# A trunk of two layers on eight cores: instructions listed a second time by due dates, squares summed on VectorE, pooling by running sums, conditioning rows ahead of x

## The chip, the cores and the metric

The kernel runs on the 8 cores of one Trainium2 chip. Each core takes one of the 8 sequences; the cores don't talk to each other. The time is the device time in microseconds (us) of the slowest core. Most executions agree within 0.3%. In some, pairs of cores, or all cores of a die, have stretches in which TensorE's granted clock is lowered, and the run is longer: 2094.3 us against 2070 for the kernel before. Below, a run is called undisturbed if no core had such a stretch; only such runs, or undisturbed cores of a run, are compared, unless the text says otherwise.

## The reference, cut to what matters

```python
for l in range(DEPTH):                                  # 2 layers; x is (8, 2048, 1024) float32
    mod = c_act @ w_mod[l] + b_mod[l]                   # shift, scale, gate for three sub-layers
    h, gate = modulate(x, norm_g[l, 0], mod_f1)         # rmsnorm(x) * g * (1 + scale) + shift
    x = x + 0.5 * gate * swiglu(h, w_ffn_in[l, 0], w_ffn_out[l, 0])    # 1024 -> 2 x 2816 -> 1024
    h, gate = modulate(x, norm_g[l, 1], mod_mx)
    y = mixer_ab(h, ...) if l % 2 == 0 else mixer_pool(h, pool_w_grp[j], pool_scale[j])
    x = x + gate * y
    h, gate = modulate(x, norm_g[l, 2], mod_f2)
    x = x + 0.5 * gate * swiglu(h, w_ffn_in[l, 1], w_ffn_out[l, 1])
return rmsnorm(x, final_g)

# mixer_pool, per channel group i with window w = 2, 4, 8, 16 (256 channels each):
p = ((cum - shifted(cum, w)) / min(t + 1, w)) - h       # trailing mean minus the token itself
outs.append(p @ w_grp[i])
```

## The kernel before

x lies transposed in SBUF (channels on partitions) as four tiles of 512 tokens. The sub-layers work on two tiles at a time, `p` = 0 and 1 in turn. The gate and up projections of the SwiGLU run as a Strassen-like scheme of 7 products, which needs sums of blocks of h ("h sums") and of the weights ("weight sums"); VectorE makes both. While one pair of tiles is in the last down projection, the next pair's h is built.

A small scheduler in the kernel decides the order. Every instruction is added with an estimated cost; on TensorE it goes behind the last one, on the other engines into the first gap that fits. Each engine is then given its instructions in the order of their planned starts, with semaphores between engines. In the traces of before, the records of VectorE (2575, accumulator reads left out) and of ScalarE (1494) stand in the order of the program on all eight cores, but for 5 memsets on VectorE whose records begin up to 0.07 us behind those of the next instruction.

```python
class Sched:
    def add(self, eng, fn, reads=(), writes=(), cost=0.1, dma=None, nbytes=0, after=0.0):
        ...                                   # dependencies from the keys read and written
        t = self.tl[e].find(ready, c)         # append for "pe", first gap for the others
        ...
    def emit(self, nc, block):
        order = sorted(ops, key=lambda o: (o.start, o.idx))
```

The norm needs the sum of squares over channels: ScalarE squares, GpSimd adds two squared channel blocks, TensorE sums over partitions with a matrix of ones. In the last down projection this follows each finished pair of channel blocks.

```python
def square_pair(c, t):
    qs = [sq_rot.next(), sq_rot.next()]
    for i, q in enumerate(qs):
        act(SQ[:, q, :], Xv(c + i, t), AF.Square, ...)
    z = sp_rot.next()
    op = add("pool", I("tensor_tensor", out=SP[:, z, :], in0=SQ[:, qs[0], :], in1=SQ[:, qs[1], :], op=ALU.add), ...)
    return z, op.end + 0.3
```

The norm factor, `rstd`, is ScalarE's Ln and Exp, just before h is built:

```python
elif nxt is not None:
    rstd(other, after=Sd.tl["pe"].tail())
    run_down(dn, rest, build_h(nxt))          # h: X * RS on VectorE, scale and shift on ScalarE, then h sums
    carry.append(lambda dn=dn: bg_add(dn.rest_ones()))
```

At the start, x comes first, then 16 rows of the first sub-layer's conditioning weights, each 128 x 1024 float32. Each is worked off on TensorE by 8 matmuls with one column (16 records in the profile):

```python
for kc in range(NC):
    op = add("pe", I("matmul", PS[b][:, i:i + 1], ap[:, kc * 128:(kc + 1) * 128], CT[:, kc:kc + 1], ...), ...)
```

The pooling multiplies h by the group's weights and then by band matrices of 128 x 128:

```python
mm(PS[bk][:, n * 128:(n + 1) * 128], GTv[:, m, dd * 128:(dd + 1) * 128], BAND0v[i] if first else BANDv[i], ...)
if not first:
    mm(PS[bk][:, n * 128:(n + 1) * 128], prev, BPREVv[i], False, True, ...)
```

In the profiles every line of the program is that of one helper (L323 before, L432 after, with other numbers in two experiments), so groups are told apart by tile names: H is h, SLOTS the weights, ACTB the hidden activations, X the residual, TP scratch, SQ and SP squares and their sums, WMOD rows of conditioning weights, RS the norm factor, ps PSUM.

## Time and profile before

| | before |
|---|---|
| time, median of the fast runs | 2070 us |
| span of the slowest core | 2066.1 us |
| TensorE busy | 1999.7 us, 97% |
| VectorE busy | 1470.1 us, 71% |
| GpSimd busy | 329.1 us, 16% |
| first feed-forward matmul, median of the cores | 81.6 us |
| from there to the start of the last projection matmul | 1962.1 us |
| from there to the end | 20.2 us |

The last three rows are read from the records of the eight cores. They cut the span into a start, a middle and an end. In the middle a second number is useful. A 512-column matmul that streams without a gap starts 0.216 us after the one before it, one of 256 columns 0.109, one of 128 columns 0.056. What the start-to-start times hold beyond that is called lost below: 43 us in the middle of the kernel before (median of the cores), 39 of them later than 12 us after the first feed-forward matmul. The first 12 us are left out because TensorE is at half clock there at first: on all eight cores of before the first matmuls start 0.43 us apart, and where the records have the stretch, a granted clock of 0.50 lasts until 84.6 to 91.1 us. Where TensorE falls back to half clock after a wait, the slower matmuls count as lost too: on core 1 of before, behind waits of 3.0, 3.3 and 4.4 us, the granted clock is 0.50 for 3.4, 3.4 and 6.8 us, and matmuls start 0.43 us apart. And where a core's record lacks matmuls (20 to 36 of them, on two cores of most profiles), each gap counts 0.216 us too much, so the ranges below leave such cores out.

### The profile page before, as it was taken

Reading aid. Unit: us, or ns where it says so; the run is one execution under the profiler, and the core shown is the slowest. Engines: PE = TensorE matmul, PEld = TensorE weight load, DVE = VectorE, ACT = ScalarE, POOL = GpSimd, SP = SyncE. Lnnn points to the kernel's source line nnn. Section 1 sums busy time; section 2 is a strip of 40 time slices with the busy share of each in tenths; the row PEclk is TensorE's granted clock in tenths of the full one; section 3 lists DMA queues with packets and bytes.
Section 4 is the critical chain, followed back from the end, with each engine's and each line's share of the span. In section 5 each row is a group of like instructions: output and inputs, shape, how many; then the busy total and the mean of one; then the engine's idle time right before and its main releaser. Section 6 shows DMA issues by size and latency. Waiting matters only on the chain.

```text
span 2066.1 us, 26542 instructions; the slowest of 8 cores (2061.0 to 2066.1 us)
## 1 busy us (share of the span) xinstructions
PE 1999.7 (97%) x9586; PEld 954.3 (46%) x9586; DVE 1470.1 (71%) x2831; ACT 922.6 (45%) x1522; POOL 329.1 (16%) x431
## 2 busy tenths in 40 slices
PE   6999999999999989999999999999999999999996
PEld 5744444444545434444444444444454445444442
DVE  2584888677888885769677976696687766685654
ACT  3351555236353453255314641464376545564242
POOL 2101221002213120012001200120012101220001
PEclk9999999999999999999999999999999999999998
DMA  8597666866575746554767485636344453436552
GB/s 256 108 226 162 136 130 145 171 134 138 131 144 124 150 80 121 141 99 87 154 136 144 102 181 140 108 62 105 59 72 81 73 98 55 84 63 111 139 86 82
DMA packets 71391, 248.78 MB, mean 120 GB/s; under 512 B 7136, under 2 KB 7264, under 8 KB 70752
## 3 DMA queue, kind: packets, MB, share of 16 engines
q0 software_dynamic: 46928, 153.63, 45.3%
q1 hardware_dynamic: 24336, 93.45, 13.5%
q8 instruction: 80, 1.31, 0.3%
q14 instruction: 47, 0.39, 0.1%
HBM read 392.29 MB, written 8.39 MB: 194 GB/s over the span
## 4 chain that ended last, share of the span: by engine, by line
PE 83%; DVE 13%; DMA 2%; POOL 1%; ACT 1%; issue 0%; SPq 0%; DVEq 0%; POOLq 0%
PE ps L323 83%; DVE X L323 4%; DVE TP L323 3%; DVE H L323 2%; DVE SLOTS L323 2%; DMA WMOD<-wmod 1%; POOL SP L323 1%; DVE WMOD L323 1%; DMA X<-xT 1%; ACT H L323 0%; ACT SQ L323 0%; DVE ps L323 0%; DVE ACTB L323 0%; ACT L323 0%; DVE MODT L323 0%
## 5 line engine op out<-in xcount | busy, mean ns | idle before, releaser
L323 PE MATMUL ps<-H,SLOTS 128*128 128x512 f16 x5440 | 1207.0, 380 | 17.5 <-DVE X L323 12.7
L323 PEld LDWEIGHTS ps<-H,SLOTS 128*128 128x128 f16 x5440 | 530.8, 98 | 653.0 <-issue 34.8
L323 PE MATMUL ps<-ACTB,SLOTS 128*128 128x512 f16 x3072 | 687.0, 380 | 3.2 <-DVE X L323 2.1
L323 ACT ACTIVATE ps<-ps 128x512 f32<-128x512 f32 x528 | 307.0, 583 | 666.2 <-PE ps L323 665.8
L323 PEld LDWEIGHTS ps<-ACTB,SLOTS 128*128 128x128 f16 x3072 | 300.8, 98 | 363.7 <-issue 9.4
L323 DVE TENSOR_TENSOR ACTB<-TP,ps 128x512 f16<-128x512 f32 x368 | 251.9, 687 | 105.4 <-PE ps L323 74.0
L323 DVE SCALAR_TENSOR_TENSOR X<-ps,GH,X 128x512 f32<-128x512 f32 x320 | 232.0, 746 | 132.4 <-PE ps L323 131.6
L323 DVE TENSOR_TENSOR SLOTS<-SLOTS 128x512 f16<-128x512 f16 x704 | 310.1, 459 | 10.8 <-DMA SLOTS<-win 0.9
L323 ACT ACTIVATE TP<-ps 128x512 f32<-128x512 f32 x400 | 238.8, 597 | 172.3 <-PE ps L323 171.9
L323 DVE TENSOR_TENSOR TP<-ps,TP 128x512 f32<-128x512 f32 x176 | 121.6, 691 | 205.9 <-ACT ps L323 205.6
L323 POOL DMA_DIRECT2D SLOTS<-win x176 | 95.3, 541 | 978.7 <-PE ps L323 923.8
L323 POOL TENSOR_TENSOR SP<-SQ 128x512 bf16<-128x512 f32 x112 | 153.3, 1373 | 252.3 <-ACT SQ L323 236.3
L323 ACT ACTIVATE SQ<-X 128x512 f32<-128x512 f32 x224 | 133.6, 622 | 118.0 <-DVE X L323 104.3
L323 DVE SCALAR_TENSOR_TENSOR WMOD<-WMOD,CB 128x512 f32<-128x512 f32 x256 | 177.6, 723 | 2.6 <-DMA WMOD<-wmod 2.5
L323 ACT ACTIVATE H<-TP,MODT,AS 128x512 f16<-128x512 f32 x160 | 122.1, 804 | 102.0 <-DVE TP L323 66.1
L323 DVE TENSOR_TENSOR ps<-ps,TP 128x512 f32<-128x512 f32 x176 | 122.9, 699 | 32.7 <-PE ps L323 32.4
L323 DVE TENSOR_TENSOR TP<-X,RS 128x512 f32<-128x512 f32 x192 | 135.9, 743 | 5.5 <-ACT H L323 4.2
L323 POOL DMA_DIRECT2D SLOTS<-wout x64 | 45.5, 710 | 334.6 <-PE ps L323 334.6
L323 PE MATMUL ps<-SP,ONES 128*128 128x512 bf16 x122 | 48.6, 417 | 29.6 <-POOL SP L323 27.1
L323 DVE TENSOR_TENSOR H<-H 128x1024 f16<-128x1024 f16 (+1 forms) x72 | 56.7, 807 | 1.6 <-ACT H L323 0.6
L323 PEld LDWEIGHTS ps<-SP,ONES 128*128 128x128 bf16 x122 | 12.5, 103 | 57.9 <-issue 49.7
L323 ACT ACT_TABLE_LOAD x28 | 35.9, 1283 | 1.5 <-PEq L329 1.1
(72 smaller groups left out, 534.2 us busy)
## 6 DMA issues: line engine op xcount, KB each, us to landing
SLOTS<-win POOLq DMA_DIRECT2D x176, 512.0 KB, 5.5
WMOD<-wmod SPq DMA_DIRECT2D x134, 512.0 KB, 5.8
SLOTS<-wout POOLq DMA_DIRECT2D x32, 768.0 KB, 7.2
SLOTS<-wout POOLq DMA_DIRECT2D x32, 640.0 KB, 6.9
SLOTS<-wab POOLq DMA_DIRECT2D x28, 512.0 KB, 7.1
X<-xT SPq DMA_DIRECT2D x4, 2048.0 KB, 16.1
outT<-X SPq DMA_DIRECT2D x16, 512.0 KB, 4.4
ACTB<-wmod SPq DMA_DIRECT2D x10, 512.0 KB, 19.1
```

Source lines behind the costliest of these rows:

```text
L323: return lambda E: getattr(E, name)(*a, **k)
```

## The change

Its intent is to start the feed-forward work earlier, to take the norm's work out of the crowded ends of the sub-layers, to have less to do on TensorE in the pooling, and to order VectorE's and ScalarE's instructions by how urgently TensorE needs them. The diff, cut to its core:

```diff
+    def relist(self, free=("dve", "act")):
+        ...
+            due.append(o.start + (0.0 if o.eng == "pe" else 8.0))
+        for o in reversed(ops):               # a due date is the earliest of the users', less cost and latency
+            ...
+        # second listing: DVE and ACT take the ready instruction with the earliest due date;
+        # PE, GpSimd and SP keep their order
     ...
-        op = add("pool", I("tensor_tensor", out=SP[:, z, :], in0=SQ[:, qs[0], :], in1=SQ[:, qs[1], :], op=ALU.add), ...)
+    def squares(c, t, n):                     # SQ is bf16 now, n squares, n/2 sums in one instruction
+        ...
+        op = tt_(SQ[:, q:q + h, :], SQ[:, q:q + h, :], SQ[:, q + h:q + n, :], ALU.add, ...)
     ...
-        for c0 in (0, 2):                     # build_h
-            for c in (c0, c0 + 4, c0 + 1, c0 + 5):
-                for tt in range(2):
+        for tt in range(2):
+            for n, c in enumerate((0, 4, 1, 5, 2, 6, 3, 7)):
     ...
-                    rstd(other, after=Sd.tl["pe"].tail())
-                    run_down(dn, rest, build_h(nxt))
-                    carry.append(lambda dn=dn: bg_add(dn.rest_ones()))
+                    run_down(dn, rest, side)  # side = build_h(nxt), begun with the end of the gate stage
+                    carry.append(lambda p=p: bg_add(stats_gen([2 * p, 2 * p + 1])))
     ...                                       # rstd: half a sub-layer earlier where possible
+    on_pe = (0, 2, 4, 6, 8, 10, 12, 14, 15)   # the other 7 rows: one scalar_tensor_tensor of 1024 columns on DVE
+    early = 6                                 # six rows are sent ahead of x
     ...
-    for s, k in zip(range(NSLOT), (0, 2, 4, 5, 6, 7)):
+    for s, k in zip(range(NSLOT), (3, 5, 6, 7, 7, 7)):    # first weight pieces
     ...                                       # pooling
-    mm(... GTv[:, m, ...], BAND0v[i] if first else BANDv[i], ...); mm(... prev, BPREVv[i], ...)
+    add("dve", I("tensor_tensor_scan", sv, PMH[:, c, cols], PMH[:, c, 16 - w + tt * TT:16 - w + (tt + 1) * TT],
+                 init, ALU.add, ALU.subtract), ...)
+    op = stt(out, PMH[:, c, cols], -float(w), sv, ALU.mult, ALU.add, ...)
+    mm(PS[bk][:], PMW[...], PMD[:, kc, tt * TT:(tt + 1) * TT], ...)      # 512 columns
```

Also, the value projection of the spatial mixer uses 512 columns in place of 256, and background work is started only while VectorE's planned backlog is under 2 us.

## The prediction

> **What bounds the kernel now.** I read the page's busy shares, then the table of stretches (5 us at the start, 50 us over the whole span), then the timeline of both ends, then the groups of instructions.
>
> ```profile
> span 2066.1 us, 26542 instructions; the slowest of 8 cores (2061.0 to 2066.1 us)
> PE 1999.7 (97%) x9586; PEld 954.3 (46%) x9586; DVE 1470.1 (71%) x2831; ACT 922.6 (45%) x1522; POOL 329.1 (16%) x431
> ```
>
> TensorE is busy 97%, so at first sight only 66 us can be won. The stretches say more (core 1; the number in brackets behind PE counts matmuls):
>
> ```profile
> 150.00:200.00 50.00, 48.64 (x226) 21.84 (x224) 25.49 (x51) 4.11 (x7) 3.38 (x6) 1.00 0.87 191
> 200.00:250.00 50.00, 46.66 (x207) 20.11 (x205) 36.32 (x71) 28.34 (x51) 14.25 (x15) 0.97 0.52 107
> 300.00:350.00 50.00, 47.05 (x210) 20.79 (x209) 45.37 (x94) 26.75 (x45) 8.65 (x10) 0.97 0.58 127
> 700.00:750.00 50.00, 42.31 (x180) 17.65 (x178) 46.34 (x74) 30.90 (x50) 15.22 (x13) 0.93 0.46 84
> 1000.00:1050.00 50.00, 50.00 (x234) 22.66 (x232) 31.74 (x67) 11.16 (x19) 4.26 (x7) 1.00 0.76 161
> 1150.00:1200.00 50.00, 46.92 (x217) 20.66 (x215) 46.86 (x91) 28.26 (x48) 11.17 (x12) 1.00 0.57 127
> ```
>
> An undisturbed stretch starts 233 to 234 matmuls in 50 us, 0.215 us each: TensorE streams without a gap. What other stretches lack is lost time. At the ends of sub-layers VectorE is busy 45 to 47 of 50 us and TensorE waits for it. The deficits (7, 26, 23, 53 and 16 above, and 4 to 12 in each of some five other stretches) come to about 175 matmuls, 38 us; with 3 us in the mixer, where widths mix, 41 us. The 53 are the boundary behind the spatial mixer.
>
> The start and the end, from the timeline:
>
> ```profile
> 12.74 2.19 ACT L323 ACTIVATE SQ<-X 128x512 f32<-128x512 f32 x4 [9.74 <-DMA X<-xT]
> 26.21 3.41 PE L323 MATMUL ps<-CT,WMOD 128*128 128x1 f32 x16
> 77.27 3.55 PE L323 MATMUL ps<-CT,WMOD 128*128 128x1 f32 x16
> 81.55 1.91 PE L323 MATMUL ps<-H,SLOTS 128*128 128x512 f16 x4
> 85.08 45.28 PE L323 MATMUL ps<-H,SLOTS 128*128 128x512 f16 x197 [1.63 <-DVE SLOTS L323]
> ...
> 2048.06 1.26 POOL L323 TENSOR_TENSOR SP<-SQ 128x512 bf16<-128x512 f32 x1 [3.27 <-ACT SQ L323]
> 2050.68 10.69 DVE L323 SCALAR_TENSOR_TENSOR X<-X,SM,RS 128x512 f32<-128x512 f32 x16 [3.36 <-ACT RS L323]
> 2052.16 9.62 SPq L323 DMA_DIRECT2D outT<-X  x8
> ```
>
> The first feed-forward matmul starts at 81.6 us. Before it TensorE is "busy" from 26 to 81 with one-column fp32 products, 16 rows of the conditioning weights at 3.4 us a row: the largest reserve, invisible in the busy share. At the end 16 final scalings run one behind another.
>
> ```profile
> 10.00:15.00 5.00, 0.00 (x0) 0.00 (x0) 0.00 (x0) 2.19 (x4) 1.03 (x1) 1.00 1.02 328
> 25.00:30.00 5.00, 4.37 (x21) 4.18 (x20) 0.65 (x3) 3.05 (x5) 1.87 (x5) 1.00 1.02 348
> 55.00:60.00 5.00, 5.00 (x26) 5.00 (x25) 1.22 (x4) 0.46 (x1) 0.00 (x0) 1.00 0.05 19
> ```
>
> The DMA engines are full until 30 us and nearly idle at 55 us: the rows wait for TensorE, not the reverse.
>
> [...] the matmuls from 81.6 us are 0.43 us apart, and core 4's granted clock is 0.50 up to 90 us. The new kernel pays this too. [...] the product of two SBUF operands below averages 743 ns, the one with a PSUM operand 691.
>
> ```profile
> L323 DVE TENSOR_TENSOR TP<-X,RS 128x512 f32<-128x512 f32 x192 | 135.9, 743 | 5.5 <-ACT H L323 4.2
> L323 POOL TENSOR_TENSOR SP<-SQ 128x512 bf16<-128x512 f32 x112 | 153.3, 1373 | 252.3 <-ACT SQ L323 236.3
> L323 DVE TENSOR_TENSOR H<-H 128x1024 f16<-128x1024 f16 x56 | 50.1, 914 | 0.7
> L323 PE MATMUL ps<-WMOD 128*128 128x256 f16 x128 | 19.2, 273 | 0.0
> L323 PE MATMUL ps<-PMC,WMOD 128*128 128x128 f16 x240 | 19.1, 219 | 0.0
> ```
>
> **The change, part by part.**
>
> *Start (rows ahead of x, 7 of 16 rows on VectorE).* TensorE's rows fall to 9 x 3.4 = 31 us, half of them while x is still arriving. The bound becomes the DMA: 16 rows of 0.52 MB, x tiles of 2 x 2.1 MB and 0.6 MB of small inputs are 13.2 MB, at the 328 GB/s of the first stretches 40 us, plus 4 us for start and landing. Two or three weight pieces, released by earlier rows, come between: each reads 1.05 MB, 3.2 us, so 6 to 9 us if all stand ahead of the last row. I take half, 4 us: last row at 48. Then its own product, 3.4 us, and scale, h and h-sum, some 3 us: first matmul near 54 in place of 81.6. Gain 27.5 us (22 to 33).
>
> *Pooling by running sums.* Started without gaps, a 512-column matmul takes 0.216 us, 256 columns 0.109, 128 columns 0.056 (start-to-start times in the trace). Removed: 128 x 0.109 + 248 x 0.056 = 27.8 us of TensorE. Added: 64 x 0.216 = 13.8. Gain 14.0 us, straight on TensorE's stream. The value projection at 512 instead of 256 columns is worth 0.2.
>
> VectorE pays: [...] 24 subtractions at 0.75, 8 at 0.43: 51 us, in two sub-layer halves.
>
> *Squares on VectorE.* GpSimd's 112 additions of 1.37 us go. VectorE gets 48 additions of 1024 columns at 0.81 to 0.91 us, about 41 us, and 8 short ones. With 7 rows at 1.35 us, less dropped constants (10) and less contention (20, guessed from 743 against 691), VectorE has about 1470 + 51 + 41 + 3 + 10 - 30 = 1545 us, 77% of the new span. It fits on average.
>
> *Background statistics, early norm, listing by due dates.* These aim at the 41 us of boundary losses. Squares and their sums leave the crowded down projection; the norm factor is computed half a sub-layer earlier; h is built tile by tile beginning some 8 us earlier; conditioning rows no longer stand in front of urgent evictions. Left over, by judgement: first sub-layer 12.4 to 4 us, feed-forward into mixer 2.8 to 2, behind the mixer 11.7 to 4 (some 34 us of VectorE work against 27.6 us of output projection, so it cannot vanish), five later boundaries 14.3 to 6. Together 41 to 16, gain 25.
>
> *End.* Listing by due date pulls the first tile's factor and its 8 scalings (8 x 0.67 = 5.3 us) before the last projection; VectorE's addition (0.43) replaces GpSimd's 1.26. About 5.5 us.
>
> Sum: 2066.1 - 27.5 - 14.2 - 25 - 5.5 = 1993.9 us of span. Times lie 3.6 us above the span (2069.66 against 2066.1): 1997 us.
>
> **Rivals.**
>
> *VectorE becomes the bound in the pooling stages.* From the down projection at 1448 to the end of the gate stage at 1565 it is busy some 77 of 117 us. 25 us of scans and subtractions and 3 of squares, with the stretch 7 us shorter, make 105 of 110. If background work is not done by then it is drained in a lump before the boundary, up to 8 us in each of two stages: about 2012.
>
> *The start's gain is given back.* Six weight pieces lay ready at 81 us before; now hardly two. From 54 to 170 us the DMA must bring weights, gate rows and the late x; it has room, but tightly. A starved first sub-layer would return 8 to 12 us: about 2008.
>
> *The list is wrong on the chip.* It reckons 0.62 us where the trace has 0.69 to 0.75. Engines run strictly in list order, so a wrong order makes new waits. Losses would stay near 40: about 2022. Against it: the old list used the same costs and lost little in steady stretches.
>
> **Range and chances.** The start may miss by 6 us, the losses by -10 to +25: 1980 to 2022 holds it 8 times in 10. 2% faster is 2028, beyond all three rivals alone; two together would reach it. Faster 0.91, same 0.08, slower 0.01.
>
> **What would show it.** Right: first feed-forward matmul at 50 to 60 us with a full DMA until then; no 128-column matmuls; stretches over 230 matmuls at the late boundaries; VectorE near 77%; fewer than 16 scalings after the last matmul. Wrong: a start later than 65 us, TensorE waiting on weight DMAs between 60 and 170 us, VectorE at 95% and over 5 us lost near either pooling stage, or as many missing matmuls at the boundaries as before.

## The result, and the profile after

| | before | after | difference |
|---|---|---|---|
| time, median | 2070.09 us | 1984.93 us | -85 us |
| start: first feed-forward matmul | 81.6 | 59.0 | -22.6 |
| middle | 1962.1 | 1910.1 | -52.0 |
| end | 20.2 | 13.2 | -7.0 |
| lost in the middle, without its first 12 us | 39.1 | 3.2 | -35.9 |

The ratio is 0.9591, with a 95% interval of 0.9572 to 0.961. Ratios here are the mean time of one kernel's fast runs over that of the other's of the same rounds, so they are not quite the ratio of the medians. The lower four rows are medians of the eight cores of the two profiled runs. Start, middle and end sum to 81.6 us and not to 85: the slowest core gains 1.6 us more than the median one, and the time lay 3.6 us above the slowest span before and 1.6 after. The middle's 52 us are these 36 us, 2 us of the first 12, and 14 us of matmuls that no longer exist.

The page of the kernel after, its span and busy shares:

```profile
span 1982.8 us, 25298 instructions; the slowest of 8 cores (1981.7 to 1982.8 us)
PE 1947.8 (98%) x9042; PEld 896.8 (45%) x9042; DVE 1462.9 (74%) x2930; ACT 909.6 (46%) x1503; POOL 171.0 (9%) x306
```

VectorE's busy time has fallen a little, although it took on scans, subtractions, squares' sums and rows. That is the first thing to explain. The table of stretches after, in the columns of the prediction's table (stretch, its length, then busy us and number of instructions of TensorE's matmuls, its weight loads, VectorE, ScalarE and GpSimd, then granted clock, share of the DMA engines, GB/s). The second line holds the boundary behind the spatial mixer, where 53 matmuls were missing, and the third a pooling stage:

```profile
650.00:700.00 50.00, 49.44 (x230) 22.25 (x229) 48.11 (x96) 31.79 (x51) 4.24 (x8) 1.00 0.66 127
700.00:750.00 50.00, 49.19 (x229) 22.12 (x227) 42.92 (x108) 24.12 (x41) 4.80 (x8) 1.00 0.91 192
1650.00:1700.00 50.00, 50.00 (x233) 22.64 (x232) 49.02 (x90) 29.16 (x49) 4.09 (x7) 1.00 0.39 67
```

Of the other stretches from 100 to 1950 us, one in the spatial mixer (550 to 600) has 230 matmuls; the rest have 232 or more, up to 257 where narrow ones are among them. VectorE may be busy 49 of 50 us without TensorE losing a single matmul: what counts is what stands first in its queue.

Both ends of the timeline after (core 2):

```profile
52.02 3.55 PE L432 MATMUL ps<-CT,WMOD 128*128 128x1 f32 x16
57.61 0.21 DVE L432 SCALAR_TENSOR_TENSOR AS<-ps,SB,SM 128x1 f32<-128x1 f32 x1
58.77 16.44 PE L432 MATMUL ps<-H,SLOTS 128*128 128x512 f16 x64
...
1972.39 0.38 PE L432 MATMUL ps<-SQ,ONES 128*128 128x512 bf16 x1 [1.84 <-DVE SQ L432]
1974.19 5.39 DVE L432 SCALAR_TENSOR_TENSOR X<-X,SM,RS 128x512 f32<-128x512 f32 x8 [1.94 <-ACT RS L432]
```

The last row's product ends at 55.6 us, but VectorE turns it into the scale only at 57.6, because other instructions stand before it in its list (it is busy 5.00 of 5 us from 55 to 60). At the end 8 scalings are left in place of 16.

The groups of instructions after, to be held against those of before (count, then busy time and mean ns of one):

```profile
L432 DVE TENSOR_TENSOR SLOTS<-SLOTS 128x512 f16<-128x512 f16 x704 | 281.2, 418 | 9.6 <-DMA SLOTS<-win 3.2
L432 DVE TENSOR_TENSOR TP<-X,RS 128x512 f32<-128x512 f32 x192 | 125.4, 682 | 14.5 <-ACT RS L432 11.8 <-ACT H L432 2.4
L432 DVE TENSOR_TENSOR H<-H 128x1024 f16<-128x1024 f16 x56 | 37.2, 681 | 0.1
L432 DVE TENSOR_TENSOR SQ<-SQ 128x1024 bf16<-128x1024 bf16 x48 | 33.0, 687 | 10.9 <-ACT SQ L432 10.7
L432 DVE TENSOR_TENSOR_SCAN WMOD<-PMH,SLAST 128x512 f32<-128x512 f16 x18 | 23.0, 1277 | 0.0
```

The same weight sums took 459 ns on average before, the same product of x and norm factor 743, the same h sum 914. Nothing in these instructions changed, only what ran beside them. The line of the weight sums before, and a place in the timeline that shows how a mean of 459 comes about:

```profile
L323 DVE TENSOR_TENSOR SLOTS<-SLOTS 128x512 f16<-128x512 f16 x704 | 310.1, 459 | 10.8 <-DMA SLOTS<-win 0.9
...
708.21 0.75 DVE L323 SCALAR_TENSOR_TENSOR X<-ps,GH,X 128x512 f32<-128x512 f32 x1
708.69 1.27 POOL L323 TENSOR_TENSOR SP<-SQ 128x512 bf16<-128x512 f32 x1 [4.15 <-ACT SQ L323]
708.87 1.37 DVE L323 TENSOR_TENSOR SLOTS<-SLOTS 128x512 f16<-128x512 f16 x1
```

The weight sum starts while GpSimd is adding, and lasts 1.37 us in place of 0.42. I went through all records of core 1. Of the 704 weight sums, 51 overlap an addition on GpSimd and take 0.95 us on average, at most 2.36; the other 653 take 0.420. The h sums of 1024 columns take 1.22 against 0.685, the products of x and factor 1.02 against 0.68, the row products 1.52 against 0.68. All of these have two operands in SBUF. Instructions with one operand in PSUM weren't held up: 0.685 overlapping against 0.687 free, and 0.743 against 0.746. Summed over the four groups, (0.53 x 51) + (0.54 x 24) + (0.33 x 34) + (0.83 x 12) = 61 us of VectorE's time before. These additions stood in the last down projection, where h is built.

These 61 us aren't the whole answer. All durations on VectorE's list of core 1, added up, rose from 1592 to 1618 us: some 99 us of new work against 63 us won in the four groups and 10 us of dropped work. The busy time counts overlapping records once, and 33 us more of them overlap now.

### The profile page after: what moved, and what is told of

Read it like the earlier page. It is cut to its first block, busy times and chain, and to the rows that moved or that the text cites. A ratio compares the mean times of both kernels' runs of the same rounds, so it can differ in the third digit from the quotient of the medians.

```text
span 1982.8 us, 25298 instructions; the slowest of 8 cores (1981.7 to 1982.8 us)
## 1 busy us (share of the span) xinstructions
PE 1947.8 (98%) x9042; PEld 896.8 (45%) x9042; DVE 1462.9 (74%) x2930; ACT 909.6 (46%) x1503; POOL 171.0 (9%) x306
## 4 chain that ended last, share of the span: by engine, by line
PE 94%; DMA 2%; DVE 2%; SPq 1%; ACT 0%; issue 0%; DVEq 0%; POOLq 0%
PE ps L432 94%; DMA ACTB<-wmod 1%; SPq L432 1%; DVE TP L432 1%; DMA WMOD<-wmod 1%; DMA SLOTS<-win 1%; DVE WMOD L432 0%; DVE ACTB L432 0%; DVE X L432 0%; DVE SLOTS L432 0%; ACT ps L432 0%; ACT H L432 0%; ACT PMH L432 0%; DVE H L432 0%; ACT RS L432 0%
## 5 line engine op out<-in xcount | busy, mean ns | idle before, releaser
L432 PE MATMUL ps<-ACTB,SLOTS 128*128 128x512 f16 x3072 | 676.2, 379 | 1.0 <-DVE ACTB L432 1.0
L432 DVE TENSOR_TENSOR SLOTS<-SLOTS 128x512 f16<-128x512 f16 x704 | 281.2, 418 | 9.6 <-DMA SLOTS<-win 3.2
L432 ACT ACTIVATE SQ<-X 128x512 bf16<-128x512 f32 x224 | 133.3, 623 | 199.0 <-DVE X L432 117.6
L432 DVE SCALAR_TENSOR_TENSOR WMOD<-WMOD,CB 128x512 f32<-128x512 f32 (+1 forms) x258 | 173.6, 690 | 7.0 <-DMA WMOD<-wmod 7.0
L432 DVE TENSOR_TENSOR TP<-X,RS 128x512 f32<-128x512 f32 x192 | 125.4, 682 | 14.5 <-ACT RS L432 11.8
L432 PE MATMUL ps<-SQ,ONES 128*128 128x512 bf16 x130 | 43.4, 422 | 14.1 <-ACT SQ L432 5.8
L432 DVE TENSOR_TENSOR SQ<-SQ 128x1024 bf16<-128x1024 bf16 (+1 forms) x56 | 36.3, 649 | 13.7 <-ACT SQ L432 13.5
L432 ACT ACTIVATE PMH<-TP,MODT,AS 128x512 f16<-128x512 f32 x32 | 25.5, 809 | 40.5 <-DVE TP L432 40.3
L432 DVE TENSOR_TENSOR H<-H 128x1024 f16<-128x1024 f16 (+1 forms) x72 | 43.4, 623 | 0.2
```

The lines of the kernel that those rows point to most:

```text
L432: return lambda E: getattr(E, name)(*a, **k)
```

## The experiments

Theory V: the boundary losses went because VectorE got its time back: GpSimd's additions no longer hold it up, and the squares left the crowded stage. Theory L: they went because of the order by due dates. The start and the pooling are tested by themselves. Where a run gave "lost", it is the middle without its first 12 us, on undisturbed cores. All runs gave correct results. The first seven kernels and a repetition ran on a chip where pairs of cores often had a stretch of lowered clock, so their ratios have wide intervals and I quote undisturbed executions; there the kernel before gave 2068.9 to 2070.1 us.

**Without the second listing.** One line is taken out of the changed kernel.

```diff
-    Sd.relist()
```

> The changed kernel without the second listing: every engine keeps the order of the first listing. Theory L (the due-date order is what removed the boundary losses of about 38 us): most of them come back, and the early last scalings go too; 2010 to 2025 us. Theory V (VectorE has room now, because GpSimd's additions no longer hold it up and the squares left the down projection): the first order does nearly as well; under 1993 us, with under 8 us lost between the first feed-forward matmul and the last projection.

Measured: 2003.7 to 2005.4 us, 20 us more than the change; ratio 0.9657 (0.954 to 0.9774). Lost 16.7 us, and the end is 20.9 us long, with 16 scalings in one piece again. Neither theory's number holds. The listing is worth some 13.5 us in the middle and 7.7 at the end, on top of everything else. But without it, 22 of the 36 us in the middle are won already.

**The second listing alone, in the kernel before.**

```diff
+    def relist(self, free=("dve", "act")): ...     # as in the change, with the links that keep Ln and Exp together
+    Sd.relist()
```

> The kernel before with nothing but the second listing added. Theory L: boundary losses fall from 41 to under 15 us and the tail by 5 us; near 2035 us. Theory V: VectorE's own load at the boundaries is the limit, which no order mends; 2055 us or more, losses of 25 us or more.

Measured: 2080.3 and 2082.6 us in the fast runs without a disturbed core, longer than before. The ratio, 0.9994 (0.9841 to 1.0147), says nothing here, because both sides contain disturbed runs. The end falls to 14.3 us as in the change, but the losses rise from 39 us to between 60 and 63. TensorE's waits over the whole run, on an undisturbed core of the profiled run (us in all, how many, the longest):

```profile
PE ps L424 <- POOL SP L424: 35.9, 20, 9.1
PE ps L424 <- ACT ps L424: 9.3, 4, 3.6
```

On the same core TensorE waited 25.3 us for GpSimd before, and not at all for ScalarE's copies in PSUM. The products of x and norm factor average 874 ns here, 743 before: the new order puts more of them beside GpSimd's additions (63 of 192, 34 before). In the middle alone, on cores with full records, TensorE's waits for VectorE fell from some 20 us to under 12. But those for GpSimd rose from 8.4 us to 17, those for ScalarE from 0 to 10, and the time at half clock from at most 14 us to at least 37. So the order does what it should for VectorE and loses more elsewhere, and theory L falls as the sole cause. That ordering by due dates pays only where the estimated costs hold would fit this, but no run tests it.

**One edit in the kernel before: the pair sums on VectorE.**

```diff
-        op = add("pool", I("tensor_tensor", out=SP[:, z, :], in0=SQ[:, qs[0], :], in1=SQ[:, qs[1], :], op=ALU.add), ...)
+        op = tt_(SP[:, z, :], SQB[:, qs[0], :], SQB[:, qs[1], :], ALU.add, [("SQ", q) for q in qs], [("SP", z)], half=True)
```

SQB is the same buffer seen as bf16; ScalarE now writes its squares in bf16 too.

> The kernel before with one edit: the pair sums of the squares (now bf16) on VectorE instead of GpSimd, 112 short additions of about 0.42 us, at their old places. If contention is the larger part: VectorE's other operations save more than the 47 us that it takes on, boundary losses fall by 10 us or more, about 2055 us. If the place of the work and the order matter more: within 6 us of 2069.

Measured: 2052.2 to 2054.2 us against 2067.6 to 2070.2 of undisturbed runs of before on the same chip, 16 us less. (The ratio, 0.9943 with 0.9878 to 1.0008, includes disturbed runs on both sides.) VectorE took on 112 additions of 424 ns, 47 us, and its busy time still fell from 1470 to 1456 us: 61 us came back. Weight sums average 421 ns, h sums 687. Lost: 22.5 to 25.4 us. The stretches of core 1 that were 53 and 16 matmuls short:

```profile
700.00:750.00 50.00, 44.70 (x199) 19.34 (x198) 44.54 (x90) 30.07 (x50) 3.17 (x6) 0.97 0.41 76
1150.00:1200.00 50.00, 50.00 (x233) 22.67 (x232) 44.56 (x99) 25.71 (x43) 4.59 (x8) 1.00 0.81 172
```

The late boundary is whole, the one behind the mixer still lacks 34. Moving work to the busier engine made that engine less busy.

The edit does two things, though: GpSimd no longer holds up VectorE, and TensorE's matmul with ones no longer waits for a slow sum. TensorE's waits before (core 1) and in this run (core 0), start and end included:

```profile
PE ps L323 <- POOL SP L323: 27.1, 25, 9.6
PE ps L323 <- DVE X L323: 14.7, 9, 4.0
...
PE ps L323 <- DVE SP L323: 19.5, 11, 9.5
PE ps L323 <- DVE X L323: 14.8, 10, 2.7
```

In the middle, on cores with full records, TensorE waited 8.3 to 8.4 us for GpSimd's sums before (these additions took 1.3 to 2.1 us on core 1), and here 0.3 us for VectorE's; for VectorE as a whole 19.0 to 20.4 before and 18.4 to 21.2 here; and it spent 10 to 14 us at half clock before, 7 here, in stretches of 3.4 or 6.8 us that come at the longest waits. So of the 15 us won in the middle some 8 are sums that come in time, and 2 or 3 the half clock. The 61 us that VectorE got back shortened TensorE's waits for it by little; what contention alone cost the old kernel isn't shown.

**Useless additions on GpSimd, beside the changed kernel.**

```diff
+        for i in range(h):
+            add("pool", I("tensor_tensor", out=JI[:, 0, :], in0=JI[:, 0, :], in1=JI[:, 1, :], op=ALU.add), reads=["JI"], writes=["JI"],
+                cost=1.15, after=Sd.tl["pe"].tail())
```

> The changed kernel with 104 useless additions on GpSimd, 128 x 512 float32, at the places where squares are summed; nothing waits for them. If contention with GpSimd's additions is what slows VectorE: its sums of two SBUF operands get slower as in the kernel before (weight sums from 418 to about 455 ns, h sums from 681 to 800 or more), VectorE's busy time rises from 1463 to 1500 us or more, and the time by 5 to 14 us. If the time of the run with sums on GpSimd came from waiting for late sums: VectorE slower, but the time within 3 us of 1985.

Measured: 2038.2 us in the one undisturbed run, 54 us more than the control beside it (1983.8 to 1984.7). The size was far beyond what I expected. VectorE's busy time rose to 1538.5 us, weight sums average 476 ns, squares' sums 1101; the h sums, at 684, were not hit. Lost: 56 us, more than in the kernel before. Nothing waits for these additions. GpSimd also issues the weight transfers, so late weights would be a rival to contention; but VectorE's idle time before its weight sums is 6.3 us on core 1, 0.2 of it put down to a DMA (after: 9.6 and 3.2). TensorE's waits in the middle rose from under 4 us to between 37 and 41, all but 0.4 us of it for VectorE. On top came 27 to 34 us at half clock, which cost about half their length; the change has none there. So it is contention and what follows from it. A place in the timeline:

```profile
275.30 8.04 POOL L432 TENSOR_TENSOR JI<-JI 128x512 f32<-128x512 f32 x5
275.71 1.48 DVE L432 TENSOR_TENSOR SLOTS<-SLOTS 128x512 f16<-128x512 f16 x1
277.12 0.68 DVE L432 TENSOR_TENSOR ps<-ps,TP 128x512 f32<-128x512 f32 x1
278.80 1.74 DVE L432 TENSOR_TENSOR SQ<-SQ 128x1024 bf16<-128x1024 bf16 x1
```

The weight sum lasts 1.48 us, the sum with a PSUM operand 0.68 as ever, the squares' sum 1.74. Since nothing holds these additions back, they come in bursts of up to five, denser than in the kernel before, so 54 us is not the price of the old additions. The old kernel paid 16 us for having its sums on GpSimd, by the run above, and only part of that through VectorE. But the run shows that an idle engine doing nothing useful can cost more than the whole gain in the middle.

**The changed kernel with its pair sums back on GpSimd.**

```diff
-        op = tt_(SQ[:, q:q + h, :], SQ[:, q:q + h, :], SQ[:, q + h:q + n, :], ALU.add, ...)
+        for i in range(h):
+            op = add("pool", I("tensor_tensor", out=SQ[:, q + i, :], in0=SQ[:, q + i, :], in1=SQ[:, q + h + i, :], op=ALU.add), ...)
```

> The changed kernel with the pair sums of the squares back on GpSimd (bf16 operands), still in the background. If GpSimd's additions are what held VectorE up before: sums of two SBUF operands on VectorE get slower again (weight sums from 418 to about 455 ns, h sums of 1024 columns from 681 towards 850 or more), VectorE's busy time stays near 1463 us or rises although 36 us of additions left it. Time: within 5 us of the changed kernel (1985) if the slack hides it, 10 us or more longer if VectorE's room is what removed the boundary losses (theory V).

Measured: 2070.96 us at best and 2127 us in the median, and in every run most or all cores had stretches of lowered clock.

> The kernel with the pair sums on GpSimd once more, because in its first runs stretches at a lowered clock lay on every core. Counted without those stretches its losses came to some 20 us more than the changed kernel's; an undisturbed run should give 1995 to 2000 us if that holds, and 1985 to 1988 if the losses were a consequence of the lowered clock.

The second time: 2125.3 to 2182.9 us, again with lowered clocks everywhere. So neither number of that expectation was met, and there is no undisturbed run of this kernel. What was measured on VectorE is as theory V has it: weight sums 477 ns, and a busy time of 1489 us although the squares' sums are gone. Core 0 of the first profile, in stretches of 10 us; the third number from the right is the granted clock:

```profile
280.00:290.00 10.00, 5.71 (x19) 2.18 (x19) 9.60 (x17) 4.53 (x10) 4.33 (x4) 0.83 0.37 92
300.00:310.00 10.00, 10.00 (x40) 4.14 (x38) 8.56 (x24) 4.58 (x8) 0.53 (x1) 0.81 0.91 194
460.00:470.00 10.00, 10.00 (x48) 4.51 (x46) 7.97 (x18) 5.73 (x10) 0.71 (x1) 1.00 0.78 131
```

At a boundary at 285 us VectorE lets TensorE wait until the clock falls to half for 3 us; from 293 us on the clock stands at 0.81 for 162 us, though TensorE has work without a gap. That costs up to 162 x 0.19 = 31 us each time, and the cores of this profile have two such stretches. One pair of cores escaped: in the third run of the first set cores 4 and 5 took 2009.7 and 2011.1 us at a mean clock of 0.98, where cores of the profiles with two stretches took 2066 to 2070 and those with four 2125, some 28 us a stretch. So this kernel without them is 28 us slower than the change, whose cores take 1982: more than the 10 us that the first expectation named as the sign of theory V, and above the 1995 to 2000 us of the second. In the middle TensorE never waits for GpSimd's sums here; it waits 22 us for VectorE (under 4 in the change) and is 14 to 24 us at half clock. I explain no difference between kernels by the stretches at 0.81; why this kernel falls into them in every run stays open.

**The norm late again, order and background kept.**

```diff
-        for tt in range(2):
-            for n, c in enumerate((0, 4, 1, 5, 2, 6, 3, 7)):
+        for c0 in (0, 2):
+            for c in (c0, c0 + 4, c0 + 1, c0 + 5):
...                                   # and rstd directly before the down projection that builds h
```

> The changed kernel with the norm factor computed just before the last down projection and h built with it, channel by channel, as before; list by due dates and background statistics stay. If the early start of h matters: 3 us or more lost again at each of seven boundaries, 1998 us or more. If the list alone suffices: under 1990 us.

Measured: 1986.5 and 1986.9 us in the undisturbed runs, lost 5.0 us. So building h earlier and tile by tile is worth about 2 us. Once VectorE has time and the right order, the head start is hardly needed.

**All 16 rows on TensorE.**

```diff
-    on_pe = (0, 2, 4, 6, 8, 10, 12, 14, 15)
+    on_pe = tuple(range(16))
```

> The changed kernel with all 16 rows of the first conditioning on TensorE (9 there in the change), the order of the transfers unchanged. If the start is bound by the DMA: first feed-forward matmul within 3 us of 59 us. If it is bound by TensorE's rows: 7 x 3.4 = 24 us of products more, of which those before x arrives are hidden; first matmul at 66 us or later, the run 7 to 15 us longer than 1985.

Measured: 2002.3 us in the one undisturbed run, 17 us more. The first feed-forward matmul starts at 65.0 to 71.9 us, median 66.4, so TensorE's rows do bound the start once there are 16 of them. The rest came later, on core 1 for instance:

```profile
121.43 1.68 DVE L432 TENSOR_TENSOR SLOTS<-SLOTS 128x512 f16<-128x512 f16 x4 [6.51 <-DMA SLOTS<-win]
123.85 6.38 PE L432 MATMUL ps<-H,SLOTS 128*128 128x512 f16 x21 [4.03 <-DVE TP L432]
```

VectorE waits 6.5 us for a weight piece, and TensorE 4 us behind it. The transfers have little room up to 130 us, as the second rival had it: in the change the DMA engines' share is 0.91 from 50 to 100 us and 1.03 from 100 to 150 (core 2). In the changed kernel itself no such wait occurs.

**x ahead of the rows again.**

```diff
-    early = 6
-    mid = 1
+    early = 0
+    mid = 0
```

> The changed kernel with x's two tiles ahead of all rows again (as before), rows still shared by TensorE and VectorE. If sending six rows ahead matters: TensorE and VectorE sit idle until x has come and all rows are worked off after it; first feed-forward matmul 6 us or more later than 59. If the start is bound by the bytes alone, which are the same: within 3 us of 59.

Measured: 1990.9 and 1992.8 us, 6 to 8 us more. The first feed-forward matmul starts at 58.4 to 64.8 us, median 62.4. This lies between the two expectations: sending rows ahead is worth 3.4 us in the median, and more on the slowest cores; on core 1, the slowest, the middle is also 4 us longer.

**The old pooling in the changed kernel.** The band matrices and their two-step products are put back as before; the diff is the reverse of the pooling part above.

> The changed kernel with the old pooling by band matrices on TensorE. By the prediction's count: 14.0 us more of matmuls on TensorE's stream, 50 us less on VectorE (scans at 1.28 and subtractions), so 1999 us, no more than 2 us of new losses. If the running sums cost TensorE waits in the pooling stages, the difference is smaller than 14 us, under 10.

Measured: 1999.0 us in both undisturbed runs, 14 us more than the change. The middle is 1924.5 us against 1910.1, 14.4 more, and lost is 3.1, as in the change. The gain of the running sums arrives whole: VectorE, at 1429.5 us here and 1462.9 with them, pays 33 us that nobody waits for.

**An attempt at a better version, and a control.**

```diff
+        if k == NC - 1:
+            dummies(8)                 # 512-column matmuls into free banks
         row0(k)
+        if k == NC - 1:
+            dummies(10)
-    for s, k in zip(range(NSLOT), (3, 5, 6, 7, 7, 7)):
+    for s, k in zip(range(NSLOT), (6, 6, 7, 7, 7, 7)):
```

> An attempt at a better version: the changed kernel with 18 idle matmuls around the last two rows, so that TensorE's clock is up when rows 14 and 15 and the first feed-forward matmuls run, and with the first weight pieces requested after the sixth channel pair instead of the third, so that they do not slow the rows. If the last rows' products and the cold clock are what is left of the start: first feed-forward matmul 3 to 5 us earlier (near 55) and 3 us of half-clock matmuls less, 1978 to 1981 us. If the transfers or VectorE set that moment: within 2 us of the changed kernel.

> The changed kernel unaltered, as a control on this chip for the runs beside it: 1984 to 1986 us where no core has a stretch at 0.81 of the clock.

Measured: the control 1983.8 to 1984.7 us in five undisturbed runs (ratio 0.9604, 0.9547 to 0.9661), the attempt 1988.5 to 1989.7, so it fails. Its mechanism works: on core 1 row 14's product takes 1.84 us in place of 3.5 and row 15's 2.28. (In the change, core 2, two rows behind eight 512-column matmuls took 3.75 us, most of it at a granted clock of 1.00; two rows at 0.50 took 6.96.) But the scale of the last row still waits until 57.48 us in VectorE's list, behind three row products of later sub-layers, and the first matmul comes no earlier (median 57.9, control 57.8). The middle is 4.5 us longer: on core 1 VectorE waits up to 2.8 us at a time for weight pieces until 80 us, and TensorE 3.6 us behind it, so the later request is paid there. The changed kernel remains the best of all that were run.

## Why the prediction was right, step by step

The time, 1985 us, lies in the range of 1980 to 2022, on the fast side of 1997. The direction was clear, the sum was 12 us too cautious, and the terms were off in both directions: the start fell 5 us short and the boundaries brought 11 more, so the closeness of the sum owes something to luck.

- **Start**: 27.5 us predicted, 22.6 measured. The reserve and its cause were right: 16 rows on TensorE again give back 7.4 us of it, x first 3.4. The step "last row at 48, its product 3.4 us, then some 3 us" was mis-sized. On core 2 the last product runs from 52.0 to 55.6, and its scale waits 2 us in VectorE's list. I had not counted that the row before the last is also on TensorE, so that two products of 3.5 us stand one behind the other after row 14 has come at 48.6. The 4 us for start and landing were an estimate; the trace of before has about as much: in its first 5 us the DMA engines' share is 0.53, some 2.4 us idle, and the smallest transfer lands 1.7 us after its issue.
- **Pooling**: 14.0 us predicted from counts and start-to-start times, 14.4 measured. For VectorE 51 us were predicted; the share of the 24 scans in it was my estimate, not shown by the trace of before, which has no scan. Measured: 49.6 us, 30.3 of them scans and 19.3 subtractions. A scan takes 1.22 us with a constant start and 1.28 with one from memory, against 0.68 to 0.75 for most others of 512 columns. VectorE's additions to the pooling hid, and the first rival fell: no loss in the pooling stages.
- **Squares on VectorE**: 41 us for 48 additions predicted, 33 measured (687 ns), because the row that I took it from, 914 ns for an h sum, was itself slowed by GpSimd.
- **Contention**: the term that was mis-sized most. "Less contention (20, guessed from 743 against 691)" measured 61 us, by the records of before and by the one-edit experiment. The difference of two means was the wrong measure: 34 of 192 instructions took 1.02 us and the rest 0.68, and the larger part sat in groups that I did not compare, weight sums and h sums. VectorE came out at 1463 us and 74%, not 1545 and 77%: of these 82 us some 41 are contention and 8 the squares, and 33 are records that overlap and count once.
- **Boundary losses**: 41 to 16 predicted, 39 to 3 measured. This is most of the 12 us. The prediction read all 41 as TensorE waiting for VectorE. The trace of before splits them: on core 1 20 us of waits for VectorE, 8 for GpSimd's sums, and 14 us at half clock, which cost about half their length. Sums on VectorE bring the 39 down to some 23 in the old kernel; all parts without the listing leave 17 us; the listing takes 13.5 of these. The parts don't simply add up: sums put back on GpSimd cost the changed kernel 28 us, the old one 16. I had credited early h and background work with a good part; the early h is worth 2 us. What the background placement of the statistics is worth by itself was not tried.
- **End**: 5.5 us predicted, 7.0 measured, by the cause named: half of the scalings now come before the last projection, and without the listing the end is 20.9 us.
- **Rivals**: the third, a list wrong on the chip, is real elsewhere. In the kernel before, the new listing adds some 20 us of waits. It did not show in the change; that its instructions nearly take what the list reckons with would explain it, but wasn't tested. One check was worded wrongly: 64 matmuls of 128 columns remain, those of the spatial mixer.

## What to carry to other kernels

Before ordering instructions more cleverly, look whether instructions of one kind have two durations, as the weight sums here had 0.42 and 0.95 us under a mean of 0.459: what held them up, GpSimd's additions, was found in the timeline. GpSimd was not free help for VectorE here: its additions of 1.4 us held up VectorE's instructions with two operands in SBUF (61 us in all) and came too late for TensorE (8 us of waits in the middle), and moving the work to the fuller engine shortened the run by 16 us. But count what the bottleneck waits for: 61 us won on VectorE meant little less waiting on TensorE in the old kernel, while in the changed one, where little else was lost, the same contention cost 28 us. A list made from estimated costs can pay, 20 us in the changed kernel, or add waits, as in the old one; try it again after each other change.

## What the runs show of the clock, and of GpSimd beside VectorE

- In the undisturbed profile of the kernel after, all eight cores ran dense matmuls at a granted clock of 1.00 from 64 us to 1973 us. The 0.81 came in two ways. In the profile with the pair sums back on GpSimd it came in stretches: on core 0 one of 162 us from 293 us on, behind 3.4 us at half clock; from 1600 to 1650 us cores 0, 1, 4 and 5 stood at 0.81 to 0.82 and the other four at 1.00. It did not come behind every fall to half clock: before has two or three on each core in the middle and no such stretch. In a few slow executions, not profiled, the mean clock of all cores of a die was near 0.81 (0.80 to 0.83 on all eight cores in the run of 2406.85 us with all rows on TensorE). What decides between these, no run here shows.
- In the kernel before, one-column float32 matmuls ran back to back for 55 us, from 26 to 81 us, and the clock stayed at 0.50 in the records of seven cores (the eighth's has no stretch there, though its first feed-forward matmuls are 0.43 us apart as well). With other matmuls around it, a row of 8 took 1.84 us in place of 3.5.
- Beside GpSimd's additions, VectorE's weight sums, with two operands in SBUF, went from 0.42 to 0.95 us; instructions with one operand in PSUM took 0.685 us beside them and 0.687 without. In the kernel before, 112 additions of 1.4 us on GpSimd held VectorE up by some 61 us; having the sums there cost the old kernel 16 us, part of it by their own lateness, and the changed one 28.
